# Placing every SBUF tile at a multiple of 128 bytes, in a transformer kernel whose products run as three 256-column matmuls per weight block

## The chip, the core and the metric

The kernel runs on one core of one Trainium2 chip. The metric is the device time of one launch in microseconds (us), as a median over runs; lower is better. Engines are named as in the profile: PE is TensorE's matmul stream, PEld its weight loads (the loads of the stationary operand), DVE is VectorE, ACT is ScalarE, POOL is GpSimd, SP is SyncE, which issues most transfers.

## What is computed

256 rows of a 2048-wide residual stream pass through two blocks, all in float32.

```python
x = x + concat(stick_breaking(q, k, v), gated_delta(q, k, v)) @ w_out   # from rmsnorm(x) @ w_in, 7184 columns
x = x + cross_attention(rmsnorm(x), rmsnorm(mem))                       # w_xq, w_xkv, w_xo
x = x + conv_ffn(rmsnorm(x))                                            # w_up to 11264, w_down from 5632
x = rmsnorm(x)
x = x + (forgetting_attention(...) * silu(gate)) @ fox_w_out            # from rmsnorm(x) @ fox_w_in, 8224 columns
x = x + (window_attention(...) * silu(gate)) @ swa_w_out                # from rmsnorm(x) @ swa_w_in, 4608 columns
return rmsnorm(x)
```

Nearly all of the arithmetic lies in the products with the eleven large weight matrices; the weights are read once each, some 370 MB.

## The kernel before, in words

The residual stands transposed in SBUF as XT, [128 partitions, 16 row tiles, 256 rows]. A product walks over its weight matrix in blocks of 256 output columns. For each block, `granules` (L221) brings up to eight 128-row tiles of the weight by one DMA into a tile `wt` (1024 KB, three buffers, issued by SP at L235). For each half of four row tiles, ACT copies the half into `wh` as float32r (L241) and DVE writes the remainder `wl` = `wt` - `wh` (L130, called at L242). So the weight is held as a high and a low part. The other operand is held in the same way: `split` (L190) writes a tile `mv` of [128, 2, 256] with the high part in `mv[:, 0]` and the low part in `mv[:, 1]`. These tiles are called `xh` where they come from the normed residual, `mix` where they hold the first block's attention outputs, `mm` for the memory, and `mv` for the other inputs of output products.

Each weight block of 128 by 128 then takes three matmuls of 256 columns: high by high, high by low, low by high. `linB` (L248) makes [features, rows]: the weight is stationary, `mv` moves.

```python
for wh, wl, i, mv, first, last in granules(w, runs, c0, first):
    for j in range(2):
        c = slice(j * P, (j + 1) * P)
        mm(ps[:, j, :], wh[:, i, c], mv[:, 0, :], first and j == 0, False)
        mm(ps[:, j, :], wh[:, i, c], mv[:, 1, :], False, False)
        mm(ps[:, j, :], wl[:, i, c], mv[:, 0, :], False, last)
```

`linA` (L259) makes [rows, features] and swaps the parts: a 128-column slice of `mv` is stationary, 256 columns of `wh` or `wl` move. All matmuls are recorded at the helper's line L119, so they are told apart by their tiles. A stationary operand of float32r is 128 columns, 512 bytes per partition; a moving one is 256 columns, 1024 bytes per partition. `tick` (L204) puts one step of the attention work of the block (scores, softmax, small products, gated delta chains) between two halves of a granule; the Tile framework orders and synchronises the engines by what reads and writes which tile.

Tiles come from pools: `cp` (constants), `wp` (`wt`, `wh`, `wl`), `xp` (`xh`), `sp` (norm pieces), and pools per stage, `gd`, `mixp`, `xa`, `mvx`, `mvf`, `mva`, `ff`, `at`. A pool packs its tiles one behind the other, each at a multiple of 32 bytes; buffers of one tag differ by their size. The first tile, `cols`, is 2628 bytes per partition, which puts what follows it at 96 bytes past a multiple of 128, and the small tiles of `sp` put what follows those at 32 past.

Of the kernel before, what the change touches and what calls it, by code (L numbers as in the profile page):

```python
# [9 lines left out]
F32 = mybir.dt.float32  # L10
F32R = mybir.dt.float32r
BF16 = mybir.dt.bfloat16
# [4 lines left out]
S, D, P = 256, 2048, 128  # L17
# [3 lines left out]
# lanes of work that runs beside the products: how many tasks at once  # L21
# [72 lines left out]
def _packed(inputs):  # L94
    """Vectors as columns of 128, and short rows for every partition: layout only."""
    inputs = dict(inputs, norm_g_2=inputs["norm_g_2"][0], norm_g_2b=inputs["norm_g_2"][1])
    parts = [np.asarray(inputs[n]).reshape(w, P).T for n, w in _COLS]
    parts += [np.broadcast_to(np.asarray(inputs[n]).reshape(1, w), (P, w)) for n, w in _ROWS]
    return np.ascontiguousarray(np.concatenate(parts, axis=1))
# [4 lines left out]

@with_exitstack
def body(ctx: ExitStack, tc: tile.TileContext, d: dict, out: bass.AP, stop=None):
# [4 lines left out]
    cp = ctx.enter_context(tc.tile_pool(name="cp", bufs=1))  # L111
    wp = ctx.enter_context(tc.tile_pool(name="wp", bufs=4))
    xp = ctx.enter_context(tc.tile_pool(name="xp", bufs=16))
    sp = ctx.enter_context(tc.tile_pool(name="sp", bufs=2))
# [59 lines left out]
    def rsqrt(dst, src, pool, tag, shape, scale, eps):  # L174
        """dst = (src * scale + eps) ** -0.5, with a Newton step."""
        n = int(np.prod(shape[1:]))
        a = pool.tile([P, n], F32, tag=tag, name="rsa", bufs=2)
        t = pool.tile([P, n], F32, tag=tag, name="rst", bufs=2)
        av, tv = a[:, :n], t[:, :n]
        if len(shape) == 3:  # L180
            av = av.rearrange("p (a b) -> p a b", a=shape[1])
            tv = tv.rearrange("p (a b) -> p a b", a=shape[1])
        vec.tensor_scalar(av, src, scale, eps, op0=ALU.mult, op1=ALU.add)
        act(dst, av, AF.Ln)
        act(dst, dst, AF.Exp, scale=-0.5)
        act(tv, dst, AF.Square)
        stt(tv, tv, -0.5, av, ALU.mult, ALU.mult)
        stt(dst, tv, 1.5, dst, ALU.add, ALU.mult)

    def split(mv, src, scale=None):  # L190
        """mv = the float32r high and low parts of src (times a column)."""
        if scale is None:
            act(mv[:, 0, :], src, AF.Copy)
            tt(mv[:, 1, :], src, mv[:, 0, :].bitcast(F32), ALU.subtract)
        else:
            act(mv[:, 0, :], src, AF.Copy, scale=scale)  # L196
            stt(mv[:, 1, :], src, scale, mv[:, 0, :].bitcast(F32), ALU.mult, ALU.subtract)

    lanes = {}
# [4 lines left out]
    def tick():  # L204
        """One step of the oldest tasks of each lane, between two pieces of a product."""
        for lane, width in WIDTH.items():
            for gen in list(lanes.get(lane, ()))[:width]:
                if next(gen, "end") == "end":
                    lanes[lane].remove(gen)
# [11 lines left out]
    def granules(w, runs, c0, first=()):  # L221
        """runs: (first row tile, moving tiles) -> high, low, index, moving tile, first, last."""
        flat = []
        for r0, mvs in runs:
            g = 0
            for n in first:
                flat.append((r0 + g, mvs[g : g + n]))
                g += n
            for g in range(g, len(mvs), KG):
                flat.append((r0 + g, mvs[g : g + KG]))  # L230
        for gi, (r, mvs) in enumerate(flat):
            wt = wp.tile([P, len(mvs), 256], F32, tag="wt", name="wt", bufs=NWT)
            assert c0 % 256 == 0
            src = w[c0 // 2 : c0 // 2 + P, r * 256 : (r + len(mvs)) * 256].rearrange("p (k n) -> p k n", n=256)
            nc.sync.dma_start(wt[:], src)  # L235
            for h in range(0, len(mvs), KC):
                n = min(KC, len(mvs) - h)
                part = [mv() if callable(mv) else mv for mv in mvs[h : h + n]]
                wh = wp.tile([P, n, 256], F32R, tag="wh", name="wh", bufs=NWC)
                wl = wp.tile([P, n, 256], F32R, tag="wl", name="wl", bufs=NWC)  # L240
                act(wh[:], wt[:, h : h + n, :], AF.Copy)  # L241
                tt(wl[:], wt[:, h : h + n, :], wh[:].bitcast(F32), ALU.subtract)  # L242
                for i in range(n):
                    last = gi == len(flat) - 1 and h + i == len(mvs) - 1
                    yield wh, wl, i, part[i], gi == 0 and h + i == 0, last
                tick()

    def linB(w, runs, c0, first=()):  # L248
        """[features, rows] of two column tiles."""
        ps = pl.tile([P, 2, 256], F32, tag="lin", name="linb")  # L250
        for wh, wl, i, mv, first, last in granules(w, runs, c0, first):
            for j in range(2):
# [4 lines that stand above are left out]
        return ps  # L257

    def linA(w, runs, c0):  # L259
        """[rows, features]"""  # L260
# [9 lines left out]
    def thin(w, g):  # L270
        """[4 partial sums of 32 features, rows]: four row tiles in four column tiles at once."""
# [10 lines left out]
    def thin_rows(thin, r, dst, name):  # L282
        """dst: [rows, features], the sum of the four, scaled by r."""
# [8 lines left out]
    class Norm:  # L292
        """Sums of squares of the residual's columns, tile by tile; then their rsqrt."""
# [21 lines left out]
        def rstd(self, wait=2):  # L315
            """rsqrt of the mean, while the next product runs."""
# [10 lines left out]
    def column(r):  # L327
        """The [rows, 1] forms of a row that all partitions hold."""
# [17 lines left out]
    def residual(w, runs, scale=None, after=None):  # L346
        """XT += product; after(k): what follows for a finished tile."""
# [25 lines left out]
    def popen(**kw):  # L373
        cm = tc.tile_pool(**kw)
        p = cm.__enter__()
# [81 lines left out]
    def small(tag):  # L457
        return gd.tile([P, 4], F32, tag=tag, name=tag, bufs=2)
# [64 lines left out]
    def chain(hp, KQ, v, sz):  # L523
        un = slice(4 * hp, 4 * hp + 4)
        g, beta, gc, bge, tail = (gates[n][:, un] for n in ("g", "beta", "gc", "bge", "tail"))

        # rows of k, v, q; the squared lengths of k's and q's
        kps, vps, qps = side([P, 4, P], "kps"), side([P, 4, P], "vps"), side([P, 4, P], "qps")
        ssk, ssq, ssw = small("ssk"), small("ssq"), small("ssw")
# [10 lines left out]
        rk, bk, ck, tk = small("rk"), small("bk"), small("ck"), small("tk")  # L540
# [9 lines left out]
        # decay, and the products with the keys  # L550
# [18 lines left out]
        cd = gd.tile([P, 8], F32, tag="cd", name="cd", bufs=2)  # L569
# [13 lines left out]
        # T = (I + L)^-1 and its transpose, chunk by chunk, by doubling blocks  # L583
# [51 lines left out]
        # the scan over chunks; rows of the output, with the halves of a block swapped  # L635
# [34 lines left out]
        # out norm: q's length and scale go into the epsilon  # L670
        m = small("m")
# [5 lines left out]
        ro = small("ro")  # L677
# [97 lines left out]
    with tc.tile_pool(name="xa", bufs=2) as xa:  # L775
# [86 lines left out]
    with tc.tile_pool(name="ff", bufs=2) as ff:  # L862
# [38 lines left out]
    # final norm of the first block, folded with the first norm of the second  # L901
# [22 lines left out]
    def softmax(zt, mask, sink=None):  # L924
        """zt: scores of [rows 1 | rows 0, one part | rows 0, the other] -> weights of [rows 0 | rows 1]."""
        nm = ap_.tile([P, 2], F32, tag="nm", name="nm", bufs=6)
        sm = ap_.tile([P, 2], F32, tag="sm", name="sm", bufs=6)
# [8 lines left out]
        if sink is not None:  # L936
            es = ap_.tile([P, 2], F32, tag="es", name="es", bufs=6)
# [18 lines left out]
    def pair(mvs, at, score, vs, gate, j, mask, sinks=(None, None)):  # L956
        """Two heads: scores, weights, transposes, and the products in the two halves of the columns."""
# [25 lines left out]
    def halves(src, tag, bufs):  # L983
        """Per head of a pair: its high part in its own rows, its low part in the other's."""
# [7 lines left out]
    def twice(src, tag, bufs):  # L992
        """Per head of a pair: its high part and its low part, each in the rows of both."""
# [14 lines left out]
    def gate2(ps, r):  # L1008
        """Twice the silu of the gate."""
# [173 lines left out]
def _blocks(w):  # L1183
    """[rows, columns] -> for each 256 columns, for each of 128 rows: its row of every row tile. Layout only."""
# [4 lines left out]
def _tail(w):  # L1189
    """The last 32 columns: for each of 128 rows, its row of every row tile. Layout only."""  # L1190
# [32 lines left out]
```

## Time and profile before

| what | value |
|---|---|
| median of 3 runs | 2257.55 us (2254.33, 2257.55, 2259.85) |
| span of the profiled execution, first to last instruction | 2253.7 us |
[...]
| PE busy | 2230.6 us, 99% of the span |
| DVE busy | 1499.4 us, 67% |
| ACT busy | 1203.9 us, 53% |
| moved by DMA | 380.69 MB, 169 GB/s |

The page gives the profiled execution's span and no time of its own beside it; the median lies 3.9 us above the span, the fastest run 0.6 us. Matmuls overlap in the records: one of 256 columns is shown as some 280 ns long, although they follow each other every 113 to 120 ns. So the mean length of one says little about the rate. The rate is read from first and last starts and counts, or from the starts in the timeline.

### The profile page before, as it was taken

To read this page: it belongs to the slowest core of one execution; us is meant where nothing else is said; L and a number is where in the kernel's file an instruction comes from. 1 tells how busy PE (TensorE), PEld (TensorE's weight loads), DVE (VectorE), ACT (ScalarE), POOL (GpSimd) and SP (SyncE) were. 2 spreads that over 40 slices of the span, in tenths; PEclk is the share of its full clock that TensorE was granted. 3 is DMA by queue.
4 is the path that set the end of the run, shared out by engine and by line. 5 is a ranking of instruction groups with operands and counts; after the bars stand their busy time and mean duration, and the time that the engine had idled before them with its cause. 6 is when DMAs were issued, how large, how long until landed. Compare 5 with 4: busy or idle time off the path is not lost.

```text
span 2253.7 us, 45530 instructions
## 1 busy us (share of the span) xinstructions
PE 2230.6 (99%) x19214; PEld 2189.6 (97%) x19214; DVE 1499.4 (67%) x2474; ACT 1203.9 (53%) x2036; POOL 119.5 (5%) x161
## 2 busy tenths in 40 slices
PE   9999999999999999999999999999999999999997
PEld 8999999999999999999999999999999999999997
DVE  7747566467587756656765778766666666787864
ACT  6544555356565534544544556555555554566662
POOL 1101010000000000000000000000110000000021
PEclk9999999999999999999999999999999999999999
DMA  7433434346565565565555556444444455444443
GB/s 266 151 131 132 134 129 142 122 153 207 165 205 178 166 202 185 171 197 187 179 175 196 187 165 213 162 165 165 166 166 167 150 188 187 156 163 150 158 163 111
DMA packets 62349, 380.69 MB, mean 169 GB/s; under 512 B 6592, under 2 KB 12864, under 8 KB 19520
## 3 DMA queue, kind: packets, MB, share of 16 engines
q1 hardware_dynamic: 60768, 375.94, 50.2%
q8 instruction: 150, 2.46, 0.4%
q10 hardware_dynamic: 1232, 1.06, 0.1%
q0 software_dynamic: 144, 0.79, 0.1%
q14 instruction: 55, 0.45, 0.1%
HBM read 375.66 MB, written 2.10 MB: 168 GB/s over the span
## 4 chain that ended last, share of the span: by engine, by line
PE 93%; DVE 3%; ACT 2%; issue 1%; DMA 0%; POOL 0%; SPq 0%; DVEq 0%; ACTq 0%; POOLq 0%
PE linb L119 78%; PE lina L119 7%; PE zps L119 2%; PE yps L119 1%; PE ptps L948 1%; DVE wl L130 1%; PE nps L119 1%; PE wsp L119 1%; PE xps L119 1%; DVE y L133 0%; ACT wh L241 0%; PE snp L119 0%; DMA wt<-in_w_in 0%; PE mps L119 0%; POOL e L466 0%
## 5 line engine op out<-in xcount | busy, mean ns | idle before, releaser
L119 PE MATMUL linb<-xh,wh 128*128 128x256 f32 x7104 | 1299.7, 285 | 3.5 <-ACT xh L196 2.7
L241 ACT ACTIVATE wh<-wt 128x1024 fp32r<-128x1024 f32 (+2 forms) x713 | 745.0, 1048 | 872.1 <-PE linb L119 725.8
L130 DVE TENSOR_TENSOR wl<-wt,wh 128x1024 fp32r<-128x1024 f32 (+2 forms) x713 | 869.6, 1222 | 457.6 <-ACT wh L241 451.8
L119 PEld LDWEIGHTS linb<-xh,wh 128*128 128x128 f32 x7104 | 1106.9, 192 | 12.7 <-issue 4.7
L119 PE MATMUL linb<-xh,wl 128*128 128x256 f32 x3552 | 1004.9, 283 | 0.0
L119 PEld LDWEIGHTS linb<-xh,wl 128*128 128x128 f32 x3552 | 680.8, 192 | 0.1
L119 PE MATMUL linb<-mv,wh 128*128 128x256 f32 x2560 | 453.3, 280 | 0.0
L119 PEld LDWEIGHTS linb<-mv,wh 128*128 128x128 f32 x2560 | 390.6, 188 | 0.5 <-issue 0.3
L119 PE MATMUL linb<-mv,wl 128*128 128x256 f32 x1280 | 357.1, 279 | 0.0
L119 PEld LDWEIGHTS linb<-mv,wl 128*128 128x128 f32 x1280 | 240.3, 188 | 0.2 <-issue 0.2
L119 PE MATMUL lina<-wh,xh 128*128 128x256 f32 x832 | 157.7, 286 | 0.0
L119 PEld LDWEIGHTS lina<-wh,xh 128*128 128x128 f32 x832 | 132.0, 192 | 0.6 <-issue 0.3
L119 PE MATMUL lina<-wl,xh 128*128 128x256 f32 x416 | 117.8, 283 | 1.0 <-DVE wl L130 1.0
L133 DVE SCALAR_TENSOR_TENSOR y<-pre,cols,y 128x256 f32<-128x256 f32 x248 | 103.3, 479 | 0.3 <-ACT y L478 0.2
L119 PE MATMUL linb<-mix,wh 128*128 128x256 f32 x512 | 89.4, 278 | 0.2
L119 PEld LDWEIGHTS lina<-wl,xh 128*128 128x128 f32 x416 | 79.7, 192 | 1.2 <-DVE wl L130 1.2
L119 PEld LDWEIGHTS linb<-mix,wh 128*128 128x128 f32 x512 | 77.5, 188 | 1.2 <-issue 0.3
L119 PE MATMUL linb<-mix,wl 128*128 128x256 f32 x256 | 71.0, 278 | 0.3 <-DVE wl L130 0.3
L130 DVE TENSOR_TENSOR pre<-linb,rstd 128x512 f32<-128x512 f32 x56 | 38.7, 692 | 41.3 <-PE linb L119 41.2
L1000 POOL CAST kd<-kd 64x512 fp32r<-64x512 f32 x32 | 36.2, 1131 | 354.9 <-ACT kd L997 353.5
L133 DVE SCALAR_TENSOR_TENSOR XT<-linb,XT 128x512 f32<-128x512 f32 x48 | 33.2, 691 | 27.0 <-PE linb L119 26.9
L866 POOL MEMSET pre<- 128x4 f32 x44 | 4.3, 103 | 868.0 <-ACT wh L241 646.0
(296 smaller groups left out, 1794.1 us busy)
## 6 DMA issues: line engine op xcount, KB each, us to landing
wt<-in_w_up SPq DMA_DIRECT2D x88, 1024.0 KB, 5.2
wt<-in_fox_w_in SPq DMA_DIRECT2D x64, 1024.0 KB, 5.1
wt<-in_w_in SPq DMA_DIRECT2D x53, 1024.0 KB, 5.1
wt<-in_swa_w_in SPq DMA_DIRECT2D x36, 1024.0 KB, 5.2
wt<-in_w_down SPq DMA_DIRECT2D x32, 1024.0 KB, 4.9
wt<-in_w_out SPq DMA_DIRECT2D x16, 1024.0 KB, 5.2
wt<-in_fox_w_out SPq DMA_DIRECT2D x16, 1024.0 KB, 5.1
wt<-in_swa_w_out SPq DMA_DIRECT2D x16, 1024.0 KB, 5.1
```

The costliest lines, as they stand in the source:

```text
L119: nc.tensor.matmul(o, lhsT, rhs, start=start, stop=stop, skip_group_check=True)
L130: vec.tensor_tensor(o, a, b, op=op)
L133: vec.scalar_tensor_tensor(o, a, s, b, op0=op0, op1=op1)
L241: act(wh[:], wt[:, h : h + n, :], AF.Copy)
L866: gps.memset(pre[:, :, 0:2], 0.0)
L948: nc.tensor.transpose(tps[:, b * P : b * P + P], p[:, b * P : b * P + P], ident)
L1000: gps.tensor_copy(st[e][other, i], st[e][own, i])
```

## The change

Every SBUF pool is wrapped in a class that rounds a tile's bytes per partition up to a multiple of 128 and returns a view of the asked size. Since the first tile starts at a multiple of 128 and each later one follows a rounded one, all tiles start at multiples of 128.

```diff
+LINE = 128
+
+class Lined:
+    def __init__(self, pool):
+        self.pool = pool
+
+    def tile(self, shape, dtype, **kw):
+        n, size = int(np.prod(shape[1:])), 2 if dtype == BF16 else 4
+        if n * size % LINE == 0:
+            return self.pool.tile(shape, dtype, **kw)
+        t = self.pool.tile([shape[0], -(-n * size // LINE) * LINE // size], dtype, **kw)[:, :n]
+        return t.rearrange("p (a b) -> p a b", a=shape[1]) if len(shape) == 3 else t
...
-    cp = ctx.enter_context(tc.tile_pool(name="cp", bufs=1))
-    wp = ctx.enter_context(tc.tile_pool(name="wp", bufs=4))
-    xp = ctx.enter_context(tc.tile_pool(name="xp", bufs=16))
-    sp = ctx.enter_context(tc.tile_pool(name="sp", bufs=2))
+    cp = Lined(ctx.enter_context(tc.tile_pool(name="cp", bufs=1)))
+    wp = Lined(ctx.enter_context(tc.tile_pool(name="wp", bufs=4)))
+    xp = Lined(ctx.enter_context(tc.tile_pool(name="xp", bufs=16)))
+    sp = Lined(ctx.enter_context(tc.tile_pool(name="sp", bufs=2)))
...
-        p = cm.__enter__()
+        p = Lined(cm.__enter__())
...
-    def small(tag):
-        return gd.tile([P, 4], F32, tag=tag, name=tag, bufs=2)
+    def smalls():
+        t = gd.tile([P, 64], F32, tag="small", name="small", bufs=2)
+        used = [0]
+        def small(n=4):
+            used[0] += n
+            assert used[0] <= 64
+            return t[:, used[0] - n : used[0]]
+        return small
...
-        nm = ap_.tile([P, 2], F32, tag="nm", name="nm", bufs=6)
-        sm = ap_.tile([P, 2], F32, tag="sm", name="sm", bufs=6)
+        stats = ap_.tile([P, 32], F32, tag="stats", name="stats", bufs=6)
+        nm, sm, es = (stats[:, 2 * i : 2 * i + 2] for i in range(3))
```

So that the many tiles of 8 and 16 bytes do not each take 128, those of one gated delta chain become slices of one tile `small`, and those of one softmax slices of one tile `stats`. The same is done for the pools `xa` and `ff`. Comments and docstrings go, which changes no instruction. In the built program every engine's instructions stand in the same order as before and wait for the same semaphores; 18351 matmuls, 2467 DVE, 1859 ACT, 166 POOL and 400 SP instructions in both. What differs is where the tiles lie. Their starts, as bytes past a multiple of 128, taken from the built programs:

| tile | before | after |
|---|---|---|
| `wt`, `wh`, `wl`, `xh`, `XT`, constants | 96 | 0 |
| `mix`, `mm`, `mv` (all moving tiles other than `xh`) | 32 | 0 |
| `kd`, `qs` (attention scores), `p`, `pT`, `v` | 32 | 0 |
| gated delta tiles `KQ`, `T`, `TT`, `X` / `kt`, `kbg`, `wq`, `O` | 32 / 96 | 0 |

Slices of 128 or 256 columns of these tiles are steps of 512 or 1024 bytes, so a matmul's operand starts at the same place in a 128-byte stretch as its tile does. The pools' order, and with it the region that each tile lies in, stays; tiles move by 160 to some 700 bytes.

## Rows read from the trace of the kernel before

**Rows 1.** The profile's page: busy time, share of the span and instructions of three engines, and the granted clock in 40 slices.
```profile
PE 2230.6 (99%) x19214; PEld 2189.6 (97%) x19214; DVE 1499.4 (67%) x2474; ACT 1203.9 (53%) x2036; POOL 119.5 (5%) x161
...
PEclk9999999999999999999999999999999999999999
```
**Rows 2.** The page's chain of work that ended last, by engine.
```profile
PE 93%; DVE 3%; ACT 2%; issue 1%; DMA 0%; POOL 0%; SPq 0%; DVEq 0%; ACTq 0%; POOLq 0%
```
**Rows 3.** Groups by line over the whole span: line, engine, operation, out<-in, partitions by elements, count | busy us, mean ns of one | idle before it and its releasers.
```profile
L119 PE MATMUL linb<-xh,wh 128*128 128x256 f32 x7104 | 1299.7, 285 | 3.5 <-ACT xh L196 2.7 <-DVE xh L133 0.6
...
L119 PE MATMUL linb<-xh,wl 128*128 128x256 f32 x3552 | 1004.9, 283 | 0.0
L130 DVE TENSOR_TENSOR wl<-wt,wh 128x1024 fp32r<-128x1024 f32 (+2 forms) x713 | 869.6, 1222 | 457.6 <-ACT wh L241 451.8 <-PE linb L119 0.5
L241 ACT ACTIVATE wh<-wt 128x1024 fp32r<-128x1024 f32 (+2 forms) x713 | 745.0, 1048 | 872.1 <-PE linb L119 725.8 <-PE lina L119 61.9 <-ACT y L871 32.3
...
L119 PE MATMUL linb<-mv,wh 128*128 128x256 f32 x2560 | 453.3, 280 | 0.0
...
L119 PE MATMUL linb<-mv,wl 128*128 128x256 f32 x1280 | 357.1, 279 | 0.0
...
L119 PE MATMUL lina<-wh,xh 128*128 128x256 f32 x832 | 157.7, 286 | 0.0
...
L119 PE MATMUL lina<-wl,xh 128*128 128x256 f32 x416 | 117.8, 283 | 1.0 <-DVE wl L130 1.0
...
L119 PE MATMUL linb<-mix,wh 128*128 128x256 f32 x512 | 89.4, 278 | 0.2
...
L119 PE MATMUL linb<-mix,wl 128*128 128x256 f32 x256 | 71.0, 278 | 0.3 <-DVE wl L130 0.3
```
**Rows 4.** The tile `xh` from 660 to 760 us (w_up): count, shortest/median/longest ns, first and last start in us.
```profile
L119 PE MATMUL linb<-xh,wh x558: 283/283/283, 659.8 to 760.0; 128*128 128x256 f32 x186
...
L119 PE MATMUL linb<-xh,wl x278: 283/283/283, 660.0 to 759.7; 128*128 128x256 f32 x139
```
**Rows 5.** The same view of the tile `mv` from 790 to 835 us (w_down).
```profile
L119 PE MATMUL linb<-mv,wh x256: 279/280/280, 789.9 to 834.9; 128*128 128x256 f32 x128
...
L119 PE MATMUL linb<-mv,wl x128: 279/279/279, 789.8 to 834.7; 128*128 128x256 f32 x128
```
**Rows 6.** The same view of the tile `mix` from 500 to 538 us (w_out).
```profile
L119 PE MATMUL linb<-mix,wh x225: 276/276/276, 499.8 to 537.8; 128*128 128x256 f32 x113
...
L119 PE MATMUL linb<-mix,wl x113: 276/276/276, 499.9 to 538.0; 128*128 128x256 f32 x113
```
**Rows 7.** The same view of the tile `mv` from 625 to 639 us (w_xo).
```profile
L119 PE MATMUL linb<-mv,wh x84: 276/276/276, 624.8 to 638.9; 128*128 128x256 f32 x84
...
L119 PE MATMUL linb<-mv,wl x42: 276/276/276, 624.9 to 638.8; 128*128 128x256 f32 x42
```
**Rows 8.** Timeline of PE in a product of `linA` with `xh` stationary: start us, us, instruction, count.
```profile
267.77 0.28 PE L119 MATMUL lina<-wl,xh 128*128 128x256 f32 x1
...
269.20 0.28 PE L119 MATMUL lina<-wl,xh 128*128 128x256 f32 x1
```
**Rows 9.** The same in a product of `linA` with `mm` stationary.
```profile
599.99 0.28 PE L119 MATMUL lina<-wl,mm 128*128 128x256 f32 x1
...
600.67 0.28 PE L119 MATMUL lina<-wl,mm 128*128 128x256 f32 x1
```
**Rows 10.** Timeline of PE in the last output product (swa_w_out), around six transposes of the softmax weights.
```profile
2142.92 0.28 PE L119 MATMUL linb<-mv,wl 128*128 128x256 f32 x1
2143.03 0.40 PE L119 MATMUL linb<-mv,wh 128*128 128x256 f32 x2
2143.27 0.28 PE L119 MATMUL linb<-mv,wl 128*128 128x256 f32 x1
2143.39 0.82 PE L948 MATMUL ptps<-cst,p 128*128 128x128 f32 x6
...
2144.27 0.28 PE L119 MATMUL linb<-mv,wl 128*128 128x256 f32 x1
2144.39 0.39 PE L119 MATMUL linb<-mv,wh 128*128 128x256 f32 x2
2144.61 0.28 PE L119 MATMUL linb<-mv,wl 128*128 128x256 f32 x1
```
**Rows 11.** Timeline of PE at six score matmuls of the window attention, in float32r with 256 columns.
```profile
1946.84 0.87 PE L119 MATMUL zps<-kd,qs 128*128 128x256 f32 x6
1947.55 0.40 PE L119 MATMUL linb<-xh,wh 128*128 128x256 f32 x2
```
**Rows 12.** The group by line of those transposes over the whole span.
```profile
L948 PE MATMUL ptps<-cst,p 128*128 128x128 f32 x192 | 27.7, 273 | 1.0 <-ACT p L941 1.0
```
**Rows 13.** Stretches of w_up, of w_down and of the window attention: length, busy us (and instructions) of PE, PEld, DVE, ACT and POOL, granted clock, DMA share, GB/s.
```profile
640.00:779.00 139.00, 139.00 (x1159) 138.95 (x1159) 100.69 (x141) 74.89 (x99) 1.13 (x11) 1.00 0.54 180
779.00:841.00 62.00, 62.00 (x528) 62.00 (x528) 35.53 (x39) 25.67 (x28) 0.10 (x1) 1.00 0.61 196
1926.00:2138.00 212.00, 212.00 (x1790) 208.29 (x1789) 167.78 (x388) 137.05 (x297) 12.96 (x8) 1.00 0.47 155
```
**Rows 14.** Who waited for whom, over the whole span: us in total, times, longest us.
```profile
ACT wh L241 <- PE linb L119: 725.8, 455, 3.1
...
ACT wh L241 <- DMA wt<-in_w_in: 9.1, 4, 3.7
```

More of the change, by code (lines that the diff above doesn't have):

```diff
@@ L524, in chain @@
         un = slice(4 * hp, 4 * hp + 4)
+        small = smalls()
         g, beta, gc, bge, tail = (gates[n][:, un] for n in ("g", "beta", "gc", "bge", "tail"))
         kps, vps, qps = side([P, 4, P], "kps"), side([P, 4, P], "vps"), side([P, 4, P], "qps")
-        ssk, ssq, ssw = small("ssk"), small("ssq"), small("ssw")
+        ssk, ssq, ssw = small(), small(), small()
         for dst, src, ss in ((kps, KQ[:, 0], ssk), (qps, KQ[:, 1], ssq), (vps, v, None)):
@@ L539, in chain @@
             vec.tensor_copy(ssw[HALF[a], :], ssq[HALF[b], :])
-        rk, bk, ck, tk = small("rk"), small("bk"), small("ck"), small("tk")
+        rk, bk, ck, tk = small(), small(), small(), small()
         rsqrt(rk[:], ssk[:], gd, "rs4", [P, 4], 1.0, 1e-6)
@@ L568, in chain @@
         act(eg[:], gb, AF.Exp)
-        cd = gd.tile([P, 8], F32, tag="cd", name="cd", bufs=2)
+        cd = small(8)
         vec.tensor_copy(cd[:], eg[:].rearrange("p u (c t) -> p (u c) t", c=2)[:, :, 63])
@@ L668, in chain @@
                 act(O[orows, u, :], pss[h][orows, :], AF.Copy)
-        m = small("m")
+        m = small()
         for u in range(4):
@@ L676, in chain @@
         tt(m[:], m[:], ssw[:], ALU.add)
-        ro = small("ro")
+        ro = small()
         rsqrt(ro[:], m[:], gd, "rs4", [P, 4], 1.0 / P, 0.0)
@@ L774, in body @@
     ymv = [None] * 4
-    with tc.tile_pool(name="xa", bufs=2) as xa:
+    with tc.tile_pool(name="xa", bufs=2) as xa_:
+        xa = Lined(xa_)
         ready = [False, False]
@@ L861, in body @@
     cw, cb = V("ffn_conv"), V("ffn_conv_bias")
-    with tc.tile_pool(name="ff", bufs=2) as ff:
+    with tc.tile_pool(name="ff", bufs=2) as ff_:
+        ff = Lined(ff_)
         def ffconv(ps, ct, tag):
@@ L936, in softmax @@
         if sink is not None:
-            es = ap_.tile([P, 2], F32, tag="es", name="es", bufs=6)
             act(es[:], nm[:], AF.Exp, bias=V("swa_sinks_2")[:, sink : sink + 1])
```

## The prediction

> **What bounds the kernel now.** I read the page's busy shares first. PE is busy 99% of the span and its weight loads 97%, DVE 67%, and the granted clock is at full speed in every slice [rows 1]. The chain that ended last is PE for 93% [rows 2]. In w_up and in w_down PE is busy for the whole stretch [rows 13], and ACT's largest wait is for PE to free `wh`, 725.8 us, while its wait for a weight transfer is 9.1 us [rows 14]. So the time is the number of matmuls times the time from one start to the next, and anything that changes that step changes the end almost one to one.
>
> The step is not what one would expect from the operation alone. It is read as last start minus first start, over the count less one. All these matmuls are 256 columns of float32r with a 128-column weight load, yet:
>
> - w_up, `xh` moving, weight stationary, both 96 bytes past a multiple of 128: 836 matmuls in 100.2 us, 120.0 ns [rows 4].
> - w_down, `mv` moving at 32, weight at 96: 384 in 45.1 us, 117.75 ns [rows 5].
> - w_out, `mix` moving at 32, weight at 96: 338 in 38.2 us, 113.4 ns [rows 6]; w_xo, the same places: 126 in 14.1 us, 113 ns [rows 7].
> - `linA`, weight moving at 96: with `xh` stationary at 96 four groups of three take 1.43 us, 119 ns [rows 8]; with `mm` stationary at 32 two groups of three take 0.68 us, 113 ns [rows 9].
>
> The last pair matters most: the same helper, the same moving tile, the same length, and only the stationary tile's place differs. And the pair of 32 and 96 has two steady values: in swa_w_out four matmuls before six transposes take 0.47 us, 117.5 ns, and three after them take 0.34 us, 113 ns [rows 10]. The step therefore is no fixed price of an operand but something that the stream of moving reads and the stream of weight reads do to each other, and it depends on where the operands start.
>
> [...]
>
> **The change part by part.** Every engine's instructions, order and waits are the same, so there is nothing added, removed or moved; packing the small tiles into `small` and `stats` adds no wait. Only the starts change, all of them to 0. Four consequences:
>
> 1. *The step of `xh` products.* 7104 + 3552 + 832 + 416 = 11904 matmuls [rows 3] at 120.0 ns. What they become, no row shows, since no full-rate matmul has both operands at a multiple of 64. [...] In between stand two rows: the best steady full-rate step, 113.4 ns [rows 6], and the densest steady stream of weight load and matmul at any rate, the transposes: six last 0.82 us, one lasts 273 ns, so (820 - 273) / 5 = 109.4 ns [rows 10, 12]. I take 109.4: it is the step of 128-column weight loads beside a moving operand that does not press on them, and an aligned moving operand should press least. Gain: 11904 x 10.6 ns = 126.2 us.
> 2. *The step of `mv` products.* 2560 + 1280 = 3840 [rows 3]; the 192 of w_xo are at 113, the other 3648 taken at 117.75. Gain: 3648 x 8.35 + 192 x 3.6 = 31.2 us.
> 3. *The step of `mix` products.* 512 + 256 = 768 [rows 3] at 113.4. Gain: 768 x 4.0 = 3.1 us.
> 4. *Other engines.* A copy to `wh` lasts 1048 ns and a remainder 1222 ns, whatever the place [rows 3]. If alignment changed these, ACT and DVE would still wait for PE. That cover gets thinner: DVE is busy 167.78 of 212 us in the window attention, 79% [rows 13], and a PE faster by a tenth brings it to some 87%. Then single `wl` tiles may come late behind a softmax. Transfers: w_down runs at 196 GB/s and 0.61 of the DMA engines [rows 13]; at 109.4 ns it needs 7% more, 0.66. I give back 5 us for late `wl` tiles (an estimate: nothing now waits there, at worst a tenth of the gain).
>
> Scores (192 of 256 columns) and the memory's products are left out, some 2 us; the float32 matmuls run at half rate and show no dependence on place. Sum: 126.2 + 31.2 + 3.1 - 5 = 155.5 us, span 2253.7 - 155.5 = 2098.2. The median of the runs lies 3.9 above that span, so the forecast is **2102 us**.
>
> [...]
>
> **The rivals.**
>
> [...]
>
> *Nothing changes.* What counts is a finer unit, of 16 or 32 bytes, in which 32 and 96 are as good as 0, and the difference between `xh` and `mv` is one of region, not of start. For it: `xh` and the weights lie together, `mv`, `mix` and `mm` elsewhere, and the change moves no tile out of its region. Against: within one region w_down shows 117.75 and w_xo 113. Time: 2257.5 us. [...] No row here shows a 16-byte effect.
>
> *Slower: equal starts are the trouble.* The step of 120.0 belongs to operands that start at the same place (96 and 96), 113 to 118 to operands that start 64 apart. Six score matmuls with both operands at 32 take 0.71 us, 118 ns [rows 11], nearer to 120 than to 113. After the change all pairs start alike: `xh` products stay at 120, and the products that were better lose it, in the residual of w_down, fox_w_out, swa_w_out, w_out and w_xo: 3648 x 2.25 + 192 x 7 + 768 x 6.6 = 14.6 us more, 2272 us. It decides if the step in w_down rises above 117.75 while that in w_up stays at 120. [...]
>
> [...]
>
> **How the numbers follow.** Chances: forecast (steps of 108 to 112 ns) 0.45; only half, with steps of 112 to 118 ns, 0.20; nothing changes 0.16; slower 0.14; below 0.05. A measurement of this kernel tells 0.3%, 6.8 us, from no change, so 2251 to 2264 counts as the same. Faster 0.70, same 0.16, slower 0.14. The range goes from 2080 (a step of some 108 ns, nothing given back) through the half gain to the upper edge of no change, 2264, which leaves out the slower rival and the bare columns, 0.19.
>
> **What the changed profile would show.** Right: in w_up a step of `xh` near 109 ns, with mean matmul lengths near 272 instead of 283 to 285; w_down and w_up alike; the same 19214 records; ACT still waiting for PE before `wh`, some 550 to 650 us. Wrong: a step of 113.4 everywhere (only half); 120.0 in w_up with 117.75 or 113 in the others (nothing); 120 in w_down too (slower). If the step falls but PE's idle time rises by more than 10 us, term 4 was too small, and the rows that wait for `wl` will say so.

## The result and the profile after

The changed kernel takes **2270.64 us** (2269.68 to 2271.79, four runs) against 2257.13 for the kernel before beside it: ratio 1.0061, 95% interval 1.0047 to 1.0075. It is slower by 13.5 us. The forecast was 2102, with a range that ended at 2264. The "slower: equal starts" rival had said 2272.

The profiled execution's span is 2269.1 us, 15.4 above that of before. The changed kernel has 17 lines more above the helpers, so matmuls stand at L136, the copy to `wh` at L258, the remainder `wl` at L147. First the page's busy times and granted clock, as in [rows 1]:

```profile
PE 2248.3 (99%) x19214; PEld 2208.0 (97%) x19214; DVE 1500.1 (66%) x2474; ACT 1203.9 (53%) x2036; POOL 119.0 (5%) x161
...
PEclk9999999999999999999999999999999999999999
```

PE is busy 17.7 us longer, with the same 19214 records, and DVE and ACT are as before. The granted clock is 0.997 in the mean, 0.998 before, and 1.00 in w_up and w_down of both, so the time is in the matmuls' own step. Now the tile views that answer to [rows 4 to 7]: count, shortest/median/longest ns, first and last start. `xh` in w_up:

```profile
L136 PE MATMUL linb<-xh,wh x557: 283/283/283, 659.8 to 759.9; 128*128 128x256 f32 x186
L136 PE MATMUL linb<-xh,wl x278: 283/283/283, 660.1 to 759.8; 128*128 128x256 f32 x139
```

835 starts in 100.1 us: 100.1 / 834 = 120.0 ns, as in [rows 4]. `mv` in w_down:

```profile
L136 PE MATMUL linb<-mv,wh x252: 283/283/283, 794.8 to 839.9; 128*128 128x256 f32 x126
L136 PE MATMUL linb<-mv,wl x125: 283/283/283, 795.1 to 839.7; 128*128 128x256 f32 x125
```

377 starts in 45.1 us: 119.9 ns, where [rows 5] gave 117.75. `mix` in w_out:

```profile
L136 PE MATMUL linb<-mix,wh x213: 283/283/283, 499.8 to 538.0; 128*128 128x256 f32 x107
L136 PE MATMUL linb<-mix,wl x106: 283/283/283, 500.1 to 537.9; 128*128 128x256 f32 x106
```

319 starts in 38.2 us: 120.1 ns, where [rows 6] gave 113.4. And `mv` in w_xo, in a stretch without a pause:

```profile
L136 PE MATMUL linb<-mv,wh x91: 283/283/283, 628.8 to 645.0; 128*128 128x256 f32 x91
L136 PE MATMUL linb<-mv,wl x45: 283/283/283, 629.0 to 644.9; 128*128 128x256 f32 x45
```

136 starts in 16.2 us: 120.0 ns, where [rows 7] gave 113. So there is one step now, 120.0, whatever the tile. Even the records' lengths tell it: 283 ns everywhere, while before they were 276, 280 or 283 with steps of 113, 118 and 120.

Summed over all steps from one large-product matmul to the next (short pauses between two of them included), read from the starts, the two traces compare like this (us):

| products | before | after | difference |
|---|---|---|---|
| `xh` moving | 1278.45 | 1278.91 | +0.5 |
| `xh` stationary | 149.45 | 149.59 | +0.1 |
| `mv` moving | 451.06 | 460.36 | +9.3 |
| `mix` moving | 88.18 | 92.88 | +4.7 |
| `mm`, either way | 44.63 | 46.10 | +1.5 |
| sum | 2011.8 | 2027.8 | +16.1 |

That is the whole of the span's 15.4: what is left of the span outside these steps is 242.0 us before and 241.3 after, so packing and rounding the small tiles cost nothing that shows. The groups of DVE and ACT that answer to [rows 3], and the wait that answers to [rows 14], show that the other engines have no part in it:

```profile
L147 DVE TENSOR_TENSOR wl<-wt,wh 128x1024 fp32r<-128x1024 f32 (+2 forms) x713 | 869.8, 1223 | 467.3 <-ACT wh L258 461.0 <-PE linb L136 2.0
L258 ACT ACTIVATE wh<-wt 128x1024 fp32r<-128x1024 f32 (+2 forms) x713 | 744.8, 1047 | 890.4 <-PE linb L136 738.7 <-PE lina L136 62.6 <-ACT y L900 32.3
```

```profile
ACT wh L258 <- PE linb L136: 738.7, 457, 3.1
```

Copy and remainder last what they did (1047 and 1223 ns), and ACT waits for PE 13 us longer than before, since PE frees `wh` later.

### The profile page after: what moved, and what is told of

Read it like the earlier page. It is cut to its first block, busy times and chain, and to the rows that moved or that the text cites. A ratio compares the mean times of both kernels' runs of the same rounds, so it can differ in the third digit from the quotient of the medians.

```text
span 2269.1 us, 45530 instructions
## 1 busy us (share of the span) xinstructions
PE 2248.3 (99%) x19214; PEld 2208.0 (97%) x19214; DVE 1500.1 (66%) x2474; ACT 1203.9 (53%) x2036; POOL 119.0 (5%) x161
## 4 chain that ended last, share of the span: by engine, by line
PE 94%; DVE 3%; ACT 2%; issue 1%; POOL 0%; DMA 0%; SPq 0%; DVEq 0%; ACTq 0%; POOLq 0%
PE linb L136 79%; PE lina L136 7%; PE zps L136 2%; PE yps L136 1%; PE ptps L976 1%; PE nps L136 1%; DVE wl L147 1%; PE wsp L136 1%; PE xps L136 1%; DVE y L150 0%; ACT wh L258 0%; PE snp L136 0%; PE mps L136 0%; POOL e L492 0%; DMA wt<-in_w_in 0%
## 5 line engine op out<-in xcount | busy, mean ns | idle before, releaser
L136 PE MATMUL linb<-xh,wh 128*128 128x256 f32 x7104 | 1300.7, 285 | 2.2 <-ACT xh L213 1.7
L258 ACT ACTIVATE wh<-wt 128x1024 fp32r<-128x1024 f32 (+2 forms) x713 | 744.8, 1047 | 890.4 <-PE linb L136 738.7
L147 DVE TENSOR_TENSOR wl<-wt,wh 128x1024 fp32r<-128x1024 f32 (+2 forms) x713 | 869.8, 1223 | 467.3 <-ACT wh L258 461.0
L136 PEld LDWEIGHTS linb<-xh,wh 128*128 128x128 f32 x7104 | 1108.4, 192 | 10.8 <-issue 4.7
L136 PE MATMUL linb<-xh,wl 128*128 128x256 f32 x3552 | 1005.9, 283 | 0.0
L136 PEld LDWEIGHTS linb<-xh,wl 128*128 128x128 f32 x3552 | 681.6, 192 | 0.1
L136 PE MATMUL linb<-mv,wh 128*128 128x256 f32 x2560 | 462.6, 283 | 0.0
L136 PEld LDWEIGHTS linb<-mv,wh 128*128 128x128 f32 x2560 | 399.3, 192 | 0.5 <-issue 0.3
L136 PE MATMUL linb<-mv,wl 128*128 128x256 f32 x1280 | 362.3, 283 | 0.0
L136 PEld LDWEIGHTS linb<-mv,wl 128*128 128x128 f32 x1280 | 245.5, 192 | 0.2 <-issue 0.2
L136 PE MATMUL lina<-wh,xh 128*128 128x256 f32 x832 | 157.9, 286 | 0.0
L136 PEld LDWEIGHTS lina<-wh,xh 128*128 128x128 f32 x832 | 132.0, 192 | 0.6 <-issue 0.3
L136 PE MATMUL lina<-wl,xh 128*128 128x256 f32 x416 | 117.9, 283 | 1.0 <-DVE wl L147 1.0
L136 PE MATMUL linb<-mix,wh 128*128 128x256 f32 x512 | 94.1, 285 | 0.2
L136 PEld LDWEIGHTS linb<-mix,wh 128*128 128x128 f32 x512 | 80.0, 192 | 1.2 <-issue 0.3
L136 PEld LDWEIGHTS lina<-wl,xh 128*128 128x128 f32 x416 | 79.7, 192 | 1.2 <-DVE wl L147 1.2
L136 PE MATMUL linb<-mix,wl 128*128 128x256 f32 x256 | 72.7, 284 | 0.3 <-DVE wl L147 0.3
L147 DVE TENSOR_TENSOR pre<-linb,rstd 128x512 f32<-128x512 f32 x56 | 38.7, 692 | 41.3 <-PE linb L136 41.2
```

Of the source, the lines that this page charges most:

```text
L136: nc.tensor.matmul(o, lhsT, rhs, start=start, stop=stop, skip_group_check=True)
L147: vec.tensor_tensor(o, a, b, op=op)
```

## The experiments

The theory after the result: the read of the next weight block and the read of the moving operand disturb each other, and how much depends on the **distance between their two starts**. The rivals: the place of each operand by itself (a moving start at 32 is good, or whole 64-byte pieces matter), and the packing of small tiles, which might cost something of its own. "Distance" is always start of the moving operand minus start of the stationary one. It is given modulo 256. In the kernel before it is 0 for `xh` and 64 for `mix`, `mm` and `mv` (192 where `mm` is the stationary one); in the changed one 0 for all of them (`mv` and weight starts differ by 256 modulo 512, `xh` and weight by 0, and both pairs show 120.0).

**1. The kernel before, with only the weights moved.** Two unused tiles of 64 bytes, ahead of `wh` and behind the weight pool, put the weights at 32 past a multiple of 128 and leave all other tiles at 96 and 32. `xh` gets the distance 64, `mix` and `mv` get 128.

```diff
+    gp_ = ctx.enter_context(tc.tile_pool(name="gapx", bufs=1))
+    gp_.tile([P, 16], F32, name="gapx")
     xp = ctx.enter_context(tc.tile_pool(name="xp", bufs=16))
...
+                if not shifted:
+                    shifted.append(wp.tile([P, 16], F32, tag="gapw", name="gapw", bufs=1))
                 wh = wp.tile([P, n, 256], F32R, tag="wh"
```

> The kernel before with wt's followers wh and wl alone moved on by 64 bytes (weights at 32 past a multiple of 128, xh still at 96, mix, mm and mv still at 32). Theory 'equal starts': the step of a matmul depends on the distance between the starts of its two operands; xh products, now 64 apart, fall from 120 to 113-118 ns, and mv and mix products, now at equal starts, rise from 117.75 and 113.4 to 120: 11904 x 2.25 to 6.6 ns less and 14.6 us more, so 2193 to 2245 us. Rival 'place of the moving operand': what counts is where the moving operand itself starts in a 128-byte stretch (32 good, 0 and 96 bad); here xh moves at 96 still, mv at 32 still: no step changes but in linA, within 6 us of 2257.

Measured: 2237.8 us (2236.37 to 2239.23), ratio to before 0.9916, interval 0.9887 to 0.9944. `xh` in w_up and `mv` in w_down:

```profile
L121 PE MATMUL linb<-xh,wh x567: 279/279/280, 660.0 to 759.9; 128*128 128x256 f32 x189
L121 PE MATMUL linb<-xh,wl x284: 279/279/279, 659.8 to 759.8; 128*128 128x256 f32 x142
```

```profile
L121 PE MATMUL linb<-mv,wh x254: 279/281/285, 789.8 to 834.9; 128*128 128x256 f32 x127
L121 PE MATMUL linb<-mv,wl x127: 279/281/285, 789.9 to 834.8; 128*128 128x256 f32 x127
```

`xh` falls from 120.0 to 100.1 / 850 = 117.8 ns although `xh` still starts 96 past a multiple of 128, and `mv` rises from 117.75 to 45.1 / 380 = 118.7 although it still starts 32 past one. The expectation had `mv` at 120, as at equal starts; its distance became 128 and not 0. The place of the moving operand in a 128-byte stretch does not decide by itself; the pair does.

**2. The changed kernel, with all moving tiles 64 past the weights.** A helper `gap` opens a pool with one unused tile ahead of `xp`, `sp` and the pools of `mix`, `mm` and `mv`; w_down's `mv` are slices that begin 64 bytes into a larger tile. The 64 holds modulo 128: modulo 256 the distance is 64 for `xh`, 192 for `mix` and for `mv` outside w_down, and in w_down the buffers alternate between the two. The tiles of the pools opened behind, those of the attention among them, move to 64 as well, in runs 7, 9 and 10 too.

```diff
+    ctx.push(gap(64).__exit__)
     xp = Lined(ctx.enter_context(tc.tile_pool(name="xp", bufs=16)))
+    ctx.push(gap(64).__exit__)
...
-    mixpool = popen(name="mixp", bufs=16)
+    mixpool = popen(before=64, name="mixp", bufs=16)
```

> The changed kernel with weights at 0 and every other float32r operand (xh, mix, mm, mv) moved to 64 past a multiple of 128. 'Equal starts': all steps 113 to 118 instead of 120, 16896 x 2.25 to 6.6 ns less, 2160 to 2233 us. Rival 'place of the moving operand': 64 is neither of the places known good (32), nothing is owed to the distance, so 120 stays and 2270 us within 7.

Measured: 2225.74 us (2222.11 to 2229.37), ratio to before 0.9862, interval 0.9822 to 0.9903. `xh` in w_up and `mix` in w_out:

```profile
L147 PE MATMUL linb<-xh,wh x567: 279/280/280, 659.8 to 759.8; 128*128 128x256 f32 x189
L147 PE MATMUL linb<-xh,wl x284: 279/279/279, 659.9 to 759.9; 128*128 128x256 f32 x142
```

```profile
L147 PE MATMUL linb<-mix,wh x207: 276/276/276, 499.9 to 535.0; 128*128 128x256 f32 x104
L147 PE MATMUL linb<-mix,wl x104: 276/276/276, 499.8 to 534.8; 128*128 128x256 f32 x104
```

`xh`, at the distance 64, takes 117.8 ns, and `mix`, at 192, 35.2 / 310 = 113.5. These are the two values of [rows 10]. Neither value belongs to one of the two distances: in the kernel before w_down shows 117.75 and w_out 113.4, both at 64, and in this run `mv` in w_xo, at 192, shows 117.8 by its starts. So 64 and 192 have two states each, also with one operand at a multiple of 128.

**3 and 4. A map of distances.** The edits of run 2 with other sizes of the gaps, one run each; the diff is run 3 against run 2. The gaps of 16 and 48 bytes that run 4 asks for come out as 32 and 64, since a pool packs at multiples of 32.

```diff
-    ctx.push(gap(64).__exit__)
+    ctx.push(gap(32).__exit__)
...
-        DOWN = (64, 64, 64, 64)
+        DOWN = (16, 48, 80, 112)
```

> A map of the step by distance between moving and stationary start, weights at 0: xh 32; mix 64; w_xo 96; the four passes of w_down 16, 48, 80, 112; fox_w_out and swa_w_out 96. 'Equal starts' with a 64-byte unit: distances below 64 behave like 0 (120), from 64 on like 64 (113 to 118). 'Equal starts' with a graded cost: steps between 120 and 113 that fall as the distance nears 64. Rival 'place': only 32 is good. A step below 113 at some distance would point to a version better than both kernels.

> The second half of the map, weights at 0: xh 96; mix 32; w_xo 16; passes of w_down 8, 64, 192, 320; fox_w_out and swa_w_out 48. If only the distance within 128 bytes counts, 64, 192 and 320 give the same step (113 to 118); if a longer stretch counts they differ. 'Equal starts' with a 64-byte unit: xh at 96 gives 113 to 118, mix at 32 gives 120; by the rival 'place', mix at 32 gives 113 and xh at 96 gives 120.

Measured: 2229.12 and 2257.73 us. `xh` in w_up at the distance 32 (run 3) and at 96 (run 4):

```profile
L147 PE MATMUL linb<-xh,wh x573: 277/278/281, 659.9 to 760.0; 128*128 128x256 f32 x191
L147 PE MATMUL linb<-xh,wl x287: 277/280/281, 659.7 to 759.8; 128*128 128x256 f32 x144
```

```profile
L147 PE MATMUL linb<-xh,wh x558: 278/280/286, 659.8 to 760.0; 128*128 128x256 f32 x186
L147 PE MATMUL linb<-xh,wl x278: 281/283/285, 660.0 to 759.8; 128*128 128x256 f32 x139
```

100.3 / 859 = 116.8 ns and 100.2 / 835 = 120.0. The mean steps, from the starts, beside those of the other runs:

| distance modulo 256 | step, ns | where |
|---|---|---|
| 0 | 120.0 | before (`xh`), after (all) |
| 32 | 117.1, a mean of 116.7 and 117.8 | run 3, `xh` (of w_up's four parts three at 116.7, one at 117.8) |
| 64 and 192 | 113.3 or 117.8 | before, runs 1, 2, 6, 7, 9, 10 |
| 96 | 120.0 | run 4, `xh` |
| 128 | 118.7 | run 1 (`mix`, `mv`), run 6 (w_down) |
| 160 | 117.4 and 118.7 | run 4, `mix` and w_xo |
| 224 | 118.3 | run 3, `mv` outside w_down |

The place of the moving operand in a 256-byte stretch does not decide by itself either: a start at 160 past a multiple of 256 took 118.7 ns in run 1 (`mv`, weights at 32) and 116.7 in run 3 (`xh` in w_up, weights at 128).

In w_down the buffers of these two runs alternate between a distance and that plus 128, so its four passes give means of two: 8 and 136 gave 120.6 ns, 16 and 144 gave 117.2, 48 and 176 gave 118.4, 80 and 208 gave 118.5, 112 and 240 gave 117.5, and 64 and 192 gave 116.3. The passes of run 4 meant for 64, 192 and 320 all alternate between these two, so they can't tell whether the step repeats after 128 bytes; run 8 does. No distance and no pair of them comes down to 109.4, and even offsets of 8 and 16 bytes change the step, so neither a unit of 64 nor one of 32 bytes describes it.

**5. One read taken away.** Products of w_up by turns: as they are; with the stationary operand read from one address (S); the moving one (M); both (SM). The matmuls and loads keep their sizes; each such operand repeats one element, so these products compute something else.

```diff
+        def still(t, c):
+            return t[:, c.start : c.start + 1].to_broadcast([P, P]) if "S" in mode else t[:, c]
+        def moving(t):
+            return t[:, 0:1].to_broadcast([P, 256]) if "M" in mode else t
```

> The changed kernel (all starts at 0), where in w_up one operand of each matmul is read from one address over and over (a zero step), by turns over its 44 products: as it is; the moving operand so; the stationary so; both. Its numbers are then not w_up's product; counts and lengths stay. If the 120 ns come from the weight load's reads meeting the moving reads, the step falls to 107-112 ns in each of the three altered kinds. If they come from the moving operand's own reads (its pieces), it falls where the moving operand is still and stays at 120 where only the stationary is. If from neither (issue, PSUM), all stay at 120.

Measured: 2245.53 us. From the timeline, the last `wl` matmul of each of five products one behind the other (start us, us); between two of these rows lie 96 matmuls, the product S first, then M, SM, and one as it is:

```profile
658.64 0.28 PE L136 MATMUL linb<-xh,wl 128*128 128x256 f32 x1
...
669.53 0.28 PE L136 MATMUL linb<-xh,wl 128*128 128x256 f32 x1
...
680.25 0.28 PE L136 MATMUL linb<-xh,wl 128*128 128x256 f32 x1
...
690.97 0.28 PE L136 MATMUL linb<-xh,wl 128*128 128x256 f32 x1
...
702.48 0.28 PE L136 MATMUL linb<-xh,wl 128*128 128x256 f32 x1
```

S: 10.89 us / 96 = 113.4 ns. M: 10.72 / 96 = 111.7. SM: 10.72 / 96 = 111.7. As it is: 11.51 / 96 = 119.9. All eleven products of each kind give the same: 113.3, 111.7, 111.7 and 119.9. This is the direct measurement of the collision. With the stationary read held still 6.5 ns of the step go, with the moving one held still 8.2, and with both no more than 8.2: 6.5 of the 8.2 ns are there only while both reads walk, and the other 1.7 whenever the moving one does. The expectation had 107 to 112 for all three kinds; S lies above that. The lowest step of this pair of instructions seen here is 111.7, and the 113.4 of S stands with the moving operand at a multiple of 128.

**6. What sets the state at 64.** All large products at the distances 64 or 192 but w_down at 128, with an extra matmul of 8 to 248 columns ahead of each w_up product.

```diff
+            if first and kick:
+                mm(ps[:, 0, :kick], wh[:, i, 0:P], mv[:, 0, :kick], True, True)
```

> Every float32r operand 64 bytes from the weights' starts (as in the run with the movers at 64), and ahead of each of the 44 products of w_up one extra matmul of 8, 16, ... 248 columns whose result the product overwrites. At a distance of 64 there were two steady steps, 113.4 and 117.8 ns. If which one holds is set by the phase in which a stream starts, some widths put whole products of 96 matmuls at 113.4 and others leave 117.8; if it is set by the operands' places, the widths change nothing and all of w_up stays at 117.8.

Measured: 2238.14 us. 43 of 44 products run at 117.8 ns, one at 113.3. From the timeline, first and last `wl` matmul of that one (extra of 104 columns) and of the next (112 columns):

```profile
838.30 0.28 PE L147 MATMUL linb<-xh,wl 128*128 128x256 f32 x1
...
848.84 0.28 PE L147 MATMUL linb<-xh,wl 128*128 128x256 f32 x1
...
849.30 0.28 PE L147 MATMUL linb<-xh,wl 128*128 128x256 f32 x1
...
859.90 0.28 PE L147 MATMUL linb<-xh,wl 128*128 128x256 f32 x1
```

The first pair has 93 steps between, 10.54 / 93 = 113.3 ns; the second 90, 10.60 / 90 = 117.8. Each state lasts its whole product. But the same width of 104 columns at 1316.8 us gave 117.8, so the width alone doesn't select it. w_down, at the distance 128, shows 118.67 here too. The trace of run 10 says when it is selected. It has 210 stretches of 20 or more steps in which only large matmuls follow each other, without a pause or another matmul between: 152 stand at 117.8 and 58 at 113.3, each from end to end, none mixed. In [rows 10] too the change falls on six transposes between the large matmuls. So in these traces the state is settled where a stretch begins and lasts until something breaks the stretch; what settles it one way or the other stays open.

**7. The changed kernel with only `xh` at equal starts.** `mix`, `mm` and `mv` get their 64 bytes back (the distance is 64, or 192 for some of w_down and where `mm` is stationary); packing, rounding and `xh` stay as in the changed kernel. The attention tiles do not stay at multiples of 128: they move to 64 with the pools.

```diff
-    mvbox[0] = mvpool = popen(name="mvx", bufs=4)
+    mvbox[0] = mvpool = popen(before=64, name="mvx", bufs=4)
```

> The changed kernel with mix, mm and mv put 64 bytes from the weights' starts again, as they were before; xh and all else at multiples of 128. If the 13 us are the steps of these products, the time is that of the kernel before, 2257 within 4 us (their share by the traces: mv 9.3, mix 4.7, mm 1.5 us). If rounding and packing the small tiles cost something of their own, it stays above 2262.

Measured: 2257.2 us (2256.12 to 2258.53), ratio to before 0.9993, interval 0.9981 to 1.0004. `xh` in w_up and `mv` in w_down:

```profile
L145 PE MATMUL linb<-xh,wh x556: 283/283/284, 659.9 to 759.8; 128*128 128x256 f32 x186
L145 PE MATMUL linb<-xh,wl x279: 283/283/284, 659.8 to 759.9; 128*128 128x256 f32 x140
```

```profile
L145 PE MATMUL linb<-mv,wh x285: 276/281/283, 789.8 to 839.9; 128*128 128x256 f32 x143
L145 PE MATMUL linb<-mv,wl x142: 279/281/283, 790.0 to 839.8; 128*128 128x256 f32 x142
```

120.0 ns and 50.1 / 426 = 117.6: the steps of w_up and w_down are those of before, and so is the time. `mix` and w_xo fell into the other state, 117.8 where the kernel before had 113.6 and 113.4, so the step sum is 2016.3 us, 4.5 above that of before and 11.5 below the changed kernel's, whose span is 12.4 longer. So the loss lies in those products, to within the 1 us by which these two differ. Outside the large products' steps every run here spends 239.6 to 243.7 us, wherever the small tiles lie, packed or not.

**8. A gap of 128 bytes.** One unused tile between the weights and everything behind them. Every tile still starts at a multiple of 128, as the change wants it, but the distance is 128 instead of 0.

```diff
+    gp = ctx.enter_context(tc.tile_pool(name="gap", bufs=1))
+    gp.tile([P, 32], F32, name="gap")
     xp = Lined(ctx.enter_context(tc.tile_pool(name="xp", bufs=16)))
```

> The changed kernel with one unused tile of 128 bytes between the weight tiles and everything behind them. Every tile still starts at a multiple of 128; moving and stationary operands of every large product now start 128 apart modulo 256 (0 before). Theory that the step follows the distance of the two starts modulo 256: the step falls from 120.0 to 118.67 ns in w_up and w_down alike, 16512 x 1.33 = 22 us less, some 2248 to 2250 us. Rival, the distance modulo 128 (or the place of each operand by itself) counts: nothing changes, step 120.0, 2270 us.

Measured: 2251.23 us (2250.11 to 2254.16, ten runs), ratio to before 0.9974, interval 0.9964 to 0.9983; 19.4 us below the changed kernel. `xh` in w_up and `mv` in w_down:

```profile
L138 PE MATMUL linb<-xh,wh x563: 279/281/285, 659.9 to 760.0; 128*128 128x256 f32 x188
L138 PE MATMUL linb<-xh,wl x282: 279/281/285, 659.8 to 759.8; 128*128 128x256 f32 x141
```

```profile
L138 PE MATMUL linb<-mv,wh x282: 279/281/285, 789.9 to 839.8; 128*128 128x256 f32 x141
L138 PE MATMUL linb<-mv,wl x142: 279/281/285, 789.7 to 839.9; 128*128 128x256 f32 x142
```

100.2 / 844 and 50.2 / 423, 118.7 ns in both. So alignment to 128 bytes is no cause in itself: with the same alignment the step is 120.0 or 118.7 by the distance. It does not repeat after 128 bytes; the two pairs named above, 0 and 256 apart, give the same 120.0. The step sum falls by 20.8 us to 2007.0, the span by 19.8, some 1 to 3 us less than was expected.

**9 and 10. Two versions for use.** `xh` 32 past the weights and the others 64 or 192 past them; and the three lines of run 8 with 64 bytes instead of 128 (`[P, 16]`).

> The changed kernel with xh 32 bytes past the weights and mix, mm and mv 64 past them. Theory of the distance: xh steps of 117.1 as with 32 in the earlier run, the other products 113.6 to 116.9 as with 64; some 2220 to 2226 us, the span some 4 us below that. If the two states at 64 fall otherwise this time, mv alone moves the result by up to 3840 x 4.4 = 17 us, and the state of each stage will say so.

> The changed kernel with one unused tile of 64 bytes between the weight tiles and everything behind them, three lines more. All moving and stationary operands of the large products are 64 apart. Theory of the distance: as in the run with all movers at 64, steps of 113.3 or 117.8 by stage, 2222 to 2230 us; the residual and the attention tiles, now at 64 too, change nothing. Rival, the attention tiles' place costs something: over 2230 us with the same steps.

Measured: 2225.04 us (2223.21 to 2227.43), ratio to before 0.9856, interval 0.9836 to 0.9875; and 2226.88 us (2225.10 to 2231.49), ratio 0.9866, interval 0.9845 to 0.9888. Both beat both kernels; between them no difference can be told. `xh` in w_up of the first:

```profile
L147 PE MATMUL linb<-xh,wh x573: 277/280/281, 659.9 to 760.0; 128*128 128x256 f32 x191
L147 PE MATMUL linb<-xh,wl x287: 277/278/281, 659.7 to 759.8; 128*128 128x256 f32 x144
```

860 starts in 100.3 us, 116.8 ns. The same view of the second:

```profile
L138 PE MATMUL linb<-xh,wh x568: 279/279/279, 659.8 to 759.9; 128*128 128x256 f32 x190
L138 PE MATMUL linb<-xh,wl x283: 280/280/280, 660.0 to 759.7; 128*128 128x256 f32 x142
```

100.1 / 850, 117.8 ns. In the second, `mix` stood at 117.7 where run 2 had 113.6 at 192, and the kernel before had 113.6 at 64: the two states again, and up to 3 us of luck in that stage alone. Both versions have the attention tiles at 64 and the residual `XT` at 0, against what was expected of the second, so the two do not compare places of those tiles.

## Why the prediction was wrong

**What bounds the kernel** was right: 99% PE in both kernels, and the step sums explain the span to within 1 us.

**Term 1, the step of `xh`, failed.** It was to fall from 120.0 to 109.4 and stayed at 120.0: +0.6 us over the two `xh` rows of the table, in place of -126.2. The 109.4 came from transposes with 128 moving columns, which are not this stream: even with both reads standing still it takes 111.7 (run 5). The prediction had the right row in hand. "The step of 120.0 belongs to operands that start at the same place (96 and 96)", says its slower rival, and equal starts are what the change makes; [rows 4] was the nearest row, and the value was taken from a farther one instead. The ground for that was the author's estimate that "an aligned moving operand should press least". The changed kernel refutes it, with 120.0 and every operand at a multiple of 128; so do run 5, with 113.4 there even with the stationary read still, and run 8, with 118.7 at the same alignment.

**Terms 2 and 3** had the wrong sign by the same mistake: `mv` +9.3 us in place of -31.2, `mix` +4.7 in place of -3.1. The products of the memory gave +1.5; they were left out together with the scores as "some 2 us", though at the prediction's own 109.4 the two would have made some 4. All these products lost the distance 64 (or 192) and took the step of equal starts. The float32 matmuls kept theirs, as said: 109 ns for 128 columns (`xt`) and 215 to 216 for 256 (`xl`), before and after, against 113 to 120 for 256 in float32r.

**Term 4** was not put to the test: PE became no faster, so no `wl` could come late. Copy and remainder kept their lengths, as said. At the 1.3% that run 10 gains, ACT still waits 706.9 us for PE, so that cover is hardly touched.

**The rivals.** "Slower: equal starts" named the mechanism, the place (w_down, the outputs, w_out, w_xo) and the sign by which to know it, 120 in w_down with 120 in w_up. Of its 14.6 us, 14.0 came, from `mv` and `mix`; `mm` and `xh` make up the rest of the 16.1 measured. What it lacked is that the distance counts rather than equality: 96 is as bad as 0, 120.0 ns in both. Its low chance, 0.14, rested on an estimate of the author's that no run shows. "Nothing changes" was right for `xh`, but not for its reason: the gaps of runs 1 and 8 move tiles by 128 bytes at most, within their regions, and change the step. (The change itself moved tiles by 32 to 1248 bytes, not by 160 to some 700: weights and `xh` by 160, `mix`, `mm` and `mv` by 352.) The argument against it, that w_down and w_xo differ within one region, was no proof either way: those were the two states of one distance. "Only half" needed 113.4 everywhere, a step that no distance tried here gives to all products. "Below" needed steps under 108 ns; a time of the bare columns by themselves is shown by no run, and the lowest step here, 111.7 (run 5), lies above 108.

**The range** ended at 2264, where "same" ends, and so left out the one rival of the other sign at 2272. With a main term for which no row showed the new value, and one row that showed the old value under just the new condition, that rival deserved at least the weight of the forecast.

**Open:** what, at the start of a stretch, selects 113.3 or 117.8 at the distances 64 and 192, and what makes the pattern over distances. A version that holds 113.3 in all 16512 of these matmuls would save some 16512 x 4.4 = 73 us more than run 10 (an estimate from the two steps, and an upper bound, since part of them is there already).

## What to carry to other kernels

Where PE is the bound and every matmul has its own weight load, read the step from first and last starts by tile, and compare tiles by the distance between their moving and stationary starts: one unused tile of 64 bytes between them was worth 1.3% here, while aligning everything cost 0.6%. Before giving a changed condition a new value, look for a row that already stands under that condition; here w_up did, and it showed that nothing was to be gained. A step that is the same for all tiles, with matmul lengths that are all alike (here 120.0 and 283), can be a sign that they share one relation of places, and one gap tests it.

## What the runs showed of the hardware

- A weight load of 128 columns and a float32r matmul of 256 columns, at the full granted clock, follow each other every 111.7 ns at best seen (moving read from one address), 113.4 with the stationary read still, and 119.9 to 120.0 with both walking from equal starts.
- In these runs the step goes with the distance of the two starts, given modulo 256 (0 and 256 gave the same 120.0): 120.0 ns at 0 and 96, 118.7 at 128, 118.3 at 224, 116.7 or 117.8 at 32, and one of two lasting states, 113.3 or 117.8, at 64 and 192. Where both tiles lie by themselves did not matter in the pairs that can be compared: (96, 96) and (0, 0) give the same 120.0, (32, 32) and (0, 0) at the distance 128 the same 118.7.
- In the kernel before a state at 64 held for 743 steps on end at 117.8 (fox_w_out) and for 693 at 113.3 (w_out); in run 6 it changed between two products 11 us long, 113.3 in one and 117.8 in the next. In run 10 it never changed inside an unbroken stretch of large matmuls (210 stretches, 152 at 117.8 and 58 at 113.3).
